# Mixer steps once per output block, with longer steps, a longer lead and one PSUM pool

## The chip, the cores and the metric

The kernel runs on one core of one Trainium2 chip. The metric is the device time of one execution in microseconds (us); lower is better. Times of the kernel before are the median of three runs.

The core's engines have short names here, as in the profile: PE is TensorE (its matmuls; PEld are its weight loads, which overlap matmuls), DVE is VectorE, ACT is ScalarE, POOL is GpSimd and SP is SyncE, which issues the DMAs. Each engine takes its instructions in a fixed order and waits at an instruction until its semaphores allow it.

## The reference

Two encoder layers over 272 rows (256 tokens and 16 learned meta tokens) of width 2048, in float32. Cut to what matters:

```python
def _layer(h, w_in, ...):
    proj = jnp.einsum('bld,dp->blp', h, w_in)
    gq, gk, gv, gr, glr, nq, nk, nv = jnp.split(proj, points, axis=-1)
    y_gla = _gla_mixer(gq, gk, gv, gr, glr, ...)      # 4 heads, both directions, gated linear attention
    y_na = _na_mixer(nq, nk, nv, na_rel_bias)         # 16 heads, windowed softmax attention
    mix = jnp.einsum('blm,md->bld', jnp.concatenate([y_gla, y_na], axis=-1), w_out)
    h = _layer_norm(DEEPNORM_ALPHA * h + mix, ln1_w, ln1_b)
    ff = jnp.einsum('blf,fd->bld', jnp.square(jax.nn.relu(jnp.einsum('bld,df->blf', h, w_ff1))), w_ff2)
    return _layer_norm(DEEPNORM_ALPHA * h + ff, ln2_w, ln2_b)
```

The meta rows are dropped from the output, so the second layer computes only 256 rows wherever it can.

## The kernel before, in words

**The large matmuls.** Nearly all the time goes to `x @ w` with weights streamed from HBM. Each product is made of three matmuls on rounded halves: high weight by high and low activation, and low weight by high activation (`three`, lines 169 to 180). A matmul has 128 output rows and 272 columns; with 256 columns, the first two are one matmul of 512. The streamed unit is a chunk of weights, 128 x 1024: DMA to `raw` (L164), ACT rounds it to `wh` (L165), DVE subtracts to get `wl` (L166). Three buffers of each rotate, and `weights` keeps one chunk ahead of the one in use. The chunk is eight k-blocks of one output block.

`by_m` (lines 208 to 223) makes one output block m after another in one PSUM bank from 16 k-blocks, which is two chunks: 48 matmuls of 272 columns. After each chunk and after the block's eviction it calls `pump`. `by_k` (lines 191 to 206) makes four blocks at once in four banks, two k-blocks for each chunk, and calls `before(k)` ahead of each chunk. The output projection starts with `by_k` over `self.y`, and there `before` is `mixed` (lines 310 to 316), which also calls `pump`.

**The mixers as generators.** Everything small is written as generators that run up to their next `yield` when `pump` steps them. `fg` holds the gates, the transposes of V, the silu of the GLA output gate, the neighbourhood attention pairs and the layer-norm sums; `bg` holds the GLA heads and the norm. `pump(fg, bg)` adds credits and does as many steps as there are whole credits. A step's instructions are traced under `issue_after(self.wl)`, which puts its DVE instructions behind the newest `wl`.

- `gla_head` (lines 467 to 573): nine levels of scores in the order 7, 0 to 6, 8. `operands(lv)` makes a level's decayed q and k on DVE (L491, L496) and ACT (L493, L495); the level's matmuls are L517 and L519, and DVE merges them into `A` under a mask (L524). The operands of a level are made one level ahead of its matmuls. Then come the meta keys (`across`, L532, L535), the outputs (L550 to L554), the mean of squares (`mean`, L788), the inverse root, the gate. It yields 16 times for a head, so about once for a level.
- `na_pair` (lines 599 to 674): two attention heads. Its parts are the scores (matmuls L610 and, in layer 0, L614) and their softmax (DVE adds L619, maximum L591, ACT exponentials L593, reciprocal L594, DVE products L597 that write `ns` and `npr`); in layer 0 the softmax of the meta queries (`nms`); the transposes of V (L631, L632); the transposes of the probabilities (L646, L647, L649) and their copies to SBUF; the output matmuls (L661, L666). There is a `yield` after each of the five.

In `layer` (lines 249 to 308) the four heads are queued in `bg` ahead of the two groups of the output gate (`ev_r`); then six groups of four blocks make the neighbourhood q, k and v (`ev_na`), a pair's three blocks one after another, and a pair is queued in `fg` when its v block is evicted. `bg` is emptied ahead of the sixth group. The last pair is queued by the last block, right ahead of the output projection's `by_k`.

**Layer norm sums.** In `tail` the output blocks are added into `acc` by `ln_part`. At block 3 it sums four blocks (L762, L763) and steps `ln_shift` once, which rounds the sum for a matmul with ones (`sp`: ACT L226, DVE L227); the next pump gives the matmul itself (`mean`, L788).

**PSUM.** Eight banks, in two pools of four: `pm` for the large products (tag `mm`) and `pb` for everything else (`bank`, tag `bg`). A pool hands out its banks in turn, in the order in which the program asks. The order of each engine's instructions is set by a list scheduler at build time, which may move an instruction past others when its own estimates say that it would wait.

Of the kernel before, what the change touches and what calls it, by code (L numbers as in the profile page):

```python
# [14 lines left out]
P = 128  # L15
# [3 lines left out]
NM = 16  # L19
# [12 lines left out]
EPS = 1e-5  # L32
TAU = 16.0
NEG = -1e30
GLA_R, GLA_NA, NORMS = 1.3, 1.1, (1.0, 0.6)
LEAD = 4
DIF = 1
HALVES = slice(0, T // 2), slice(T // 2, T)


# [13 lines left out]
class Trunk:  # L54
    def __init__(self, ctx, tc, ins, out):
        self.ctx, self.tc, self.nc = ctx, tc, tc.nc
        self.i, self.out = ins, out
        self.bg, self.fg, self.credit, self.fcredit = deque(), deque(), 0, 0
        self.x = [None] * DC
        self.stream, self.ready = self.order(), deque()  # L60
        pool = lambda name, **k: ctx.enter_context(tc.tile_pool(name=name, **k))
        self.cp = pool("const", bufs=1)
        self.xp = pool("xhl", bufs=1)
        self.yp = pool("yhl", bufs=1)
        self.wp = pool("wst", bufs=3)
        self.jp = pool("jn", bufs=1)
        self.pm = pool("pm", bufs=4, space=PSUM)
        self.pb = pool("pb", bufs=4, space=PSUM)

    def bank(self):  # L70
        return self.pb.tile([P, 512], F32, name="bg", tag="bg")

    def consts(self):
        nc, c = self.nc, self.cp
# [130 lines left out]
                                      start=j + p == 0, stop=j == nk - 1 and p == 2)  # L205
        return [p[:, :n] for p in ps]

    def by_m(self, acts, ns, evict, pump=(0, 0), apart=False, renew=False):

        nk = len(acts)  # L210
        for m, n in enumerate(ns):
            ps = self.pm.tile([P, 512], F32, name="mm", tag="mm")
            for k in range(nk):
                if k % 8 == 0:
                    wh, wl = self.weights()
                self.three(ps, wh, wl, (k % 8) * P, acts[k], n, k == 0, k == nk - 1)
                if k % 8 == 7 and k < nk - 1:
                    self.pump(*pump)
                if renew and m == len(ns) - 1 and k == 8:
                    self.renew(2)  # L220
            parts = [ps[:, :T], ps[:, T:]] if n == T else [ps[:, :n]]
            evict(m, parts if apart else self.whole(parts))
            self.pump(*pump)
# [25 lines left out]
    def layer(self, l):  # L249
        nc, tc = self.nc, self.tc  # L250
        self.l = l
        self.full = l + 1 < DEPTH
        self.n = n = L if self.full else T
        with ExitStack() as actx:
            pool = lambda name, side, ctx=actx, bufs=1: ctx.enter_context(
                tc.tile_pool(name=name, bufs=bufs, side=side, reuse_waits="tile"))
            a = pool("att", "left")
            t = lambda nm, s: a.tile(s, F32, name=nm, tag=nm)
            self.qk = [t(f"qk{h}", [P, 2, L]) for h in range(GH)]
            self.be = [t(f"be{h}", [P, 2, L + 1]) for h in range(GH)]  # L260
            self.nb = [t(f"nb{h}", [P, 4]) for h in range(GH)]
            self.V = [t(f"V{i}", [P, GH * GDV]) for i in range(2)]
            self.VS = a.tile([80, GH * GDV], F32R, name="VS", tag="VS")
            nc.gpsimd.memset(self.VS.bitcast(F32), 0.0)
            self.y, self.gate, self.done = [None] * DC, {}, set()
            if l:
                self.by_m(self.x, [L + 2] * 4, lambda m, ps: self.fixed(self.ev_k, m, ps), pump=(1, NORMS[0]),
                          renew=True)
                first = self.by_k(self.x, L, self.normed)
                self.drain()  # L270
                self.lctx.close()
            else:
                with ExitStack() as ectx:
                    self.xr = pool("xr", "right", ectx)
                    for m, ps in enumerate(self.by_k(self.x, L, self.load_x, fine=True)):
                        self.ev_k(m, ps)
            with ExitStack() as ectx:
                self.ep = pool("early", "right", ectx)
                self.fcredit = 0
                self.fg.append(self.gates())  # L280
                if l == 0:
                    self.by_m(self.x, [L] * 4, self.ev_v, pump=(1, 0))
                else:
                    for m, ps in enumerate(first):
                        self.ev_v(m, ps)
                self.by_m(self.x, [n] * 4, self.ev_q, pump=(1, 0))
                self.by_m(self.x, [L] * 4, lambda m, ps: self.ev_v(4 + m, ps), pump=(1, 0))
                self.drain()
            self.a2 = pool("na", "left", bufs=2)
            with ExitStack() as gctx:  # L290
                self.credit = 0
                self.g2 = pool("gla", "right", gctx, 2)
                for h in range(GH):
                    self.bg.append(self.gla_head(h))
                for g in range(2):
                    self.by_m(self.x, [n] * 4, lambda m, ps: self.ev_r(4 * g + m, ps), pump=(1, GLA_R))
                self.na_tiles()
                for g in range(6):
                    if g == 5:
                        while self.bg:  # L300
                            self.step(self.bg, 1)
                        gctx.close()
                        self.ln_open()
                    ns = [n if (4 * g + m) % 3 == 0 else L for m in range(4)]
                    self.by_m(self.x, ns, lambda m, ps: self.ev_na(4 * g + m, ps), pump=(1, GLA_NA))
            ps = self.by_k(self.y, n, self.mixed)
            self.drain()
        self.tail(ps)
# [157 lines left out]

    def gla_head(self, h):
        nc, n, full, g2 = self.nc, self.n, self.full, self.g2
        be, qk = self.be[h], self.qk[h]
        bf, eb = be[:, 0, 1:], be[:, 1, :]  # L470
        A = g2.tile([P, 6, P], F32, name="A", tag="A")
        Am = g2.tile([NM, L], F32, name="Am", tag="Am")
        level = lambda: g2.tile([P, 2, L], F32, name="lev", tag="lev", bufs=3)

        def flat(t):

# [30 lines left out]
            return t  # L507

        order = (7, 0, 1, 2, 3, 4, 5, 6, 8)
        ahead = operands(order[0])  # L510
        for at, lv in enumerate(order):
            q, k = ahead
            ahead = operands(order[at + 1]) if at + 1 < len(order) else across()
            ps = self.bank()
            for b in (slice(0, P), slice(P, T)):
                r = b if lv < 8 else slice(P - b.start, T - b.start)
                nc.tensor.matmul(ps[:, b], lhsT=k[:, b], rhs=q[:, r], start=True, stop=True)  # L517
            if full and lv <= 4:
                nc.tensor.matmul(ps[:, T:L], lhsT=k[:, T:T + P], rhs=q[:, T:L], start=True, stop=True)  # L519
            p2 = ps[:, :T].rearrange("p (s c) -> p s c", s=2)  # L520
            if lv >= 7:
                nc.scalar.copy(A[:, 0:5:4, :] if lv == 7 else A[:, 1:4:2, :], p2)
            else:
                nc.vector.copy_predicated(A[:, 0:5:4, :], self.mask[:, lv:lv + 1, :].to_broadcast([P, 2, P]), p2)  # L524
            if full and lv == 0:
                nc.vector.tensor_copy(Am[:, T:L], ps[:NM, T:L])
            elif full and lv <= 4:
                nc.vector.copy_predicated(Am[:, T:L], self.mask[:NM, lv, :NM], ps[:NM, T:L])
            yield
        t = ahead  # L530
        ps = self.bank()
        nc.tensor.matmul(ps[:, :T], lhsT=flat(t)[:, T:T + P], rhs=t[:, 1, :T], start=True, stop=True)  # L532
        if full:
# [2 lines left out]
                                 rhs=t[:, 1, T:L], start=True, stop=True)  # L536
            nc.vector.tensor_copy(A[:, 2:6:3, :NM], ps[:, T:T + 2 * NM].rearrange("p (s c) -> p s c", s=2))
        nc.scalar.copy(Am[:, :T], ps[:NM, :T])
        yield
        am = g2.tile([80, L], F32R, name="am", tag="am")[:, :n]  # L540
        nc.gpsimd.memset(am.bitcast(F32), 0.0)
        self.stack(Am[:, :n], am, NM, (0, 64), 32)
        yield
        af = A.rearrange("p s c -> p (s c)")
        os_ = []
# [19 lines left out]
        for e in range(2):  # L565
# [7 lines left out]
            yield  # L573

    def na_tiles(self):

# [22 lines left out]
    def na_pair(self, c, q, k, v):  # L599
# [24 lines left out]
        yield  # L624
# [15 lines left out]
        yield  # L640
# [509 lines left out]
```

## Time and profile before

| | |
|---|---|
| median of 3 runs | 2365.45 us (2365.10 to 2365.86) |
| the profiled execution | 2365.56 us |
| its span, first to last instruction | 2363.8 us |
| PE busy | 2339.4 us, 99% of the span, 17354 matmuls |
| PEld busy | 2228.2 us, 94% |
| DVE busy | 1570.9 us, 66% |
| ACT busy | 1239.3 us, 52% |
| granted TensorE clock, mean | 0.998 |

The times outside the span are 1.76 us. The profile's page gives busy shares for each engine and a chain of waits followed back from the end; the timeline gives each instruction's start, duration, engine, line, tiles and, in brackets, the idle time ahead of it with what ended it. Matmuls are pipelined, so the distance between two starts, not the duration, is what one costs. The two stages with the mixers' background steps lie at about 114 to 360 us (layer 0) and 1313 to 1553 us (layer 1).

### The profile page before, as it was taken

The page shows a single profiled execution, that of the slowest core. Times are in us where ns is not written, and L with a number is a line of the kernel's source. Part 1 is how long each engine was busy: PE and PEld are TensorE (multiplying, and loading weights), DVE is VectorE, ACT ScalarE, POOL GpSimd, SP SyncE. Part 2 cuts the span into 40 slices and gives each one's busy share as a digit, 9 for nine tenths or more (in the row PEclk, how much of TensorE's full clock was granted, in tenths as well). Part 3 has the DMA queues.
Part 4 walks back from the last instruction along what each step waited for, and adds up shares of the span by engine and source line. Part 5 has one row for each costly group of instructions (what it writes and reads, how often), then busy time and mean ns, then how long its engine had stood idle before and what let it go on. Part 6 is the DMA issues. An engine that isn't in the chain of part 4 may idle for free.

```text
span 2363.8 us, 43168 instructions
## 1 busy us (share of the span) xinstructions
PE 2339.4 (99%) x17354; PEld 2228.2 (94%) x17354; DVE 1570.9 (66%) x2474; ACT 1239.3 (52%) x2251; POOL 109.8 (5%) x181
## 2 busy tenths in 40 slices
PE   9999999999999999999999999999999999999997
PEld 8999999999999999999999899998988888888887
DVE  6697777785544455547577887768866555666656
ACT  6566665564433344444456677655654333444444
POOL 1100010020000000000021000000200000000001
PEclk9999999999999999999999999999999999999999
DMA  7544445555555555556556454456566666666664
GB/s 250 165 136 150 152 141 161 176 179 181 179 179 179 180 181 181 181 179 179 179 173 190 150 157 148 147 157 199 183 193 194 196 191 193 195 193 192 195 193 137
DMA packets 120425, 417.47 MB, mean 177 GB/s; under 512 B 13405, under 2 KB 18397, under 8 KB 120225
## 3 DMA queue, kind: packets, MB, share of 16 engines
q1 hardware_dynamic: 120224, 414.72, 56.5%
q8 instruction: 136, 2.23, 0.4%
q14 instruction: 65, 0.52, 0.1%
HBM read 412.57 MB, written 2.10 MB: 175 GB/s over the span
## 4 chain that ended last, share of the span: by engine, by line
PE 95%; DVE 3%; ACT 1%; issue 1%; DMA 0%; SPq 0%; ACTq 0%; DVEq 0%
PE mm L174 21%; PE mm L178 17%; PE mm L179 17%; PE mm L180 17%; PE mm L175 11%; PE mm L204 6%; PE bg L517 2%; PE bg L661 1%; DVE wl L166 1%; PE bg L610 0%; ACT wh L165 0%; PE bg L550 0%; PE bg L351 0%; PE mm L943 0%; PE mm L958 0%
## 5 line engine op out<-in xcount | busy, mean ns | idle before, releaser
L166 DVE TENSOR_TENSOR wl<-raw,wh 128x1024 fp32r<-128x1024 f32 (+1 forms) x764 | 931.2, 1219 | 638.0 <-ACT wh L165 625.8
L165 ACT CAST wh<-raw 128x1024 fp32r<-128x1024 f32 (+1 forms) x764 | 796.5, 1043 | 929.7 <-PE mm L179 378.3
L178 PE MATMUL mm<-x,wh 128*128 128x272 f32 (+2 forms) x2176 | 622.5, 286 | 0.0
L179 PE MATMUL mm<-x,wh 128*128 128x272 f32 (+2 forms) x2176 | 618.6, 284 | 0.0
L180 PE MATMUL mm<-x,wl 128*128 128x272 f32 (+2 forms) x2176 | 617.7, 284 | 0.1
L179 PEld LDWEIGHTS mm<-x,wh 128*128 128x128 f32 x2176 | 408.7, 188 | 0.1
L178 PEld LDWEIGHTS mm<-x,wh 128*128 128x128 f32 x2176 | 407.7, 187 | 1.1 <-issue 0.5
L180 PEld LDWEIGHTS mm<-x,wl 128*128 128x128 f32 x2176 | 407.7, 187 | 0.5 <-DVE wl L166 0.3
L174 PE MATMUL mm<-x,wh 128*128 128x512 f32 x1152 | 396.8, 390 | 0.0
L175 PE MATMUL mm<-x,wl 128*128 128x256 f32 x1152 | 318.6, 277 | 0.0
L174 PEld LDWEIGHTS mm<-x,wh 128*128 128x128 f32 x1152 | 216.3, 188 | 45.2 <-issue 0.6
L174 PE MATMUL mm<-y,wh 128*128 128x512 f32 x672 | 230.5, 388 | 0.7 <-ACT wh L165 0.7
L175 PEld LDWEIGHTS mm<-x,wl 128*128 128x128 f32 x1152 | 216.2, 188 | 0.0
L178 PE MATMUL mm<-y,wh 128*128 128x272 f32 x704 | 199.2, 283 | 0.0
L179 PE MATMUL mm<-y,wh 128*128 128x272 f32 x704 | 199.2, 283 | 0.0
L180 PE MATMUL mm<-y,wl 128*128 128x272 f32 x704 | 198.9, 283 | 0.0
L175 PE MATMUL mm<-y,wl 128*128 128x256 f32 x672 | 184.5, 275 | 0.7 <-DVE wl L166 0.7
L174 PE MATMUL mm<-u,wh 128*128 128x512 f32 x480 | 164.6, 388 | 0.0
L174 PEld LDWEIGHTS mm<-y,wh 128*128 128x128 f32 x672 | 126.1, 188 | 27.1 <-ACT wh L165 1.2
L178 PE MATMUL mm<-u,wh 128*128 128x272 f32 x512 | 144.9, 283 | 0.0
L179 PE MATMUL mm<-u,wh 128*128 128x272 f32 x512 | 144.9, 283 | 0.0
L180 PE MATMUL mm<-u,wl 128*128 128x272 f32 x512 | 144.7, 283 | 0.0
(262 smaller groups left out, 3272.1 us busy)
## 6 DMA issues: line engine op xcount, KB each, us to landing
raw<-in_wff SPq DMA_DIRECT2D x512, 512.0 KB, 3.6
raw<-in_win SPq DMA_DIRECT2D x190, 512.0 KB, 3.6
raw<-in_wout SPq DMA_DIRECT2D x64, 512.0 KB, 3.6
nb<-in_nab SPq DMA_DIRECT2D x16, 352.0 KB, 3.2
xraw<-in_xT SPq DMA_DIRECT2D x7, 272.0 KB, 5.0
out<-acc SPq DMA_DIRECT2D x7, 256.0 KB, 2.4
wraw<-in_wup SPq DMA_DIRECT2D x2, 392.0 KB
raw<-in_win SPq DMA_DIRECT2D x4, 128.0 KB, 2.8
```

Source lines behind the costliest of these rows:

```text
L165: nc.scalar.copy(wh[:, c], raw[:, c])
L166: self.wl = nc.vector.tensor_tensor(wl[:, c], raw[:, c], wh[:, c].bitcast(F32), ALU.subtract).ins
L174: mm(ps, lhsT=wh[:, c:c + P], rhs=x.joined, start=first, stop=False)
L175: mm(ps[:, T:], lhsT=wl[:, c:c + P], rhs=xh[:, :T], start=False, stop=last)
L178: mm(o, lhsT=wh[:, c:c + P], rhs=xh[:, :n], start=first, stop=False)
L179: mm(o, lhsT=wh[:, c:c + P], rhs=xl[:, :n], start=False, stop=False)
L180: mm(o, lhsT=wl[:, c:c + P], rhs=xh[:, :n], start=False, stop=last)
L204: self.nc.tensor.matmul(ps[m][:, :n], lhsT=parts[p][0][:, c:c + P], rhs=acts[j][parts[p][1]][:, :n], start=j + p == 0, stop=j == nk - 1 an ...
L517: nc.tensor.matmul(ps[:, b], lhsT=k[:, b], rhs=q[:, r], start=True, stop=True)
L661: nc.tensor.matmul(r[hs], lhsT=(v2 if rest else v1)[:, t, hs], rhs=p2[:, t, :] if rest else p1[:, 2 * t + hh, :], start=rest, stop=not rest)
```

## The change

- `by_m` gets `whole`: with it there is no pump after a block's first chunk, only the one after its eviction. The eight groups of the mixer stages use it, with `pump=(1, 1)`: one step of `fg` and one of `bg` for each block.
- Steps are longer. A GLA head yields 7 times instead of 16: four steps of two levels each, one with the last level, `across` and the meta scores, one with the outputs and the sums of squares, one with the mean, the root and both gated outputs. `na_pair` yields 3 times instead of 5: scores with all the softmax; transposes of V and of the probabilities; outputs.
- Operands are made for two levels at a time, at the end of the step ahead of the one that uses them; the first two of head 0 ahead of the first group, those of the next head within the fifth step of a head. One generator for the heads chains to the next (`yield from head`).
- `lev` gets 4 buffers and `dif` 2; `A`, `Am` and `am` get 1.
- The two PSUM pools become one pool of eight banks with one tag.

The diff, cut:

```diff
-GLA_R, GLA_NA, NORMS = 1.3, 1.1, (1.0, 0.6)
+NORMS = 1.0, 0.6
-DIF = 1
+DIF = 2
...
-        self.pm = pool("pm", bufs=4, space=PSUM)
-        self.pb = pool("pb", bufs=4, space=PSUM)
+        self.pm = pool("pm", bufs=8, space=PSUM)
 
     def bank(self):
-        return self.pb.tile([P, 512], F32, name="bg", tag="bg")
+        return self.pm.tile([P, 512], F32, name="bg", tag="mm")
...
-    def by_m(self, acts, ns, evict, pump=(0, 0), apart=False, renew=False):
+    def by_m(self, acts, ns, evict, pump=(0, 0), apart=False, renew=False, whole=False):
...
-                if k % 8 == 7 and k < nk - 1:
+                if k % 8 == 7 and k < nk - 1 and not whole:
                     self.pump(*pump)
...
-                for h in range(GH):
-                    self.bg.append(self.gla_head(h))
+                head = self.gla_head(0)
+                next(head)
+                self.bg.append(head)
                 for g in range(2):
-                    self.by_m(self.x, [n] * 4, lambda m, ps: self.ev_r(4 * g + m, ps), pump=(1, GLA_R))
+                    self.by_m(self.x, [n] * 4, lambda m, ps: self.ev_r(4 * g + m, ps), pump=(1, 1), whole=True)
...
-                    self.by_m(self.x, ns, lambda m, ps: self.ev_na(4 * g + m, ps), pump=(1, GLA_NA))
+                    self.by_m(self.x, ns, lambda m, ps: self.ev_na(4 * g + m, ps), pump=(1, 1), whole=True)
...
         order = (7, 0, 1, 2, 3, 4, 5, 6, 8)
-        ahead = operands(order[0])
+        ahead = [operands(lv) for lv in order[:2]]
+        yield
...
         for at, lv in enumerate(order):
-            q, k = ahead
-            ahead = operands(order[at + 1]) if at + 1 < len(order) else across()
+            q, k = ahead.pop(0)
             ps = self.bank()
...
-            yield
-        t = ahead
+            if not ahead and at < 8:
+                ahead = [operands(order[i]) if i < 9 else across() for i in (at + 1, at + 2)]
+                yield
+        t = ahead.pop()
...
         self.stack(Am[:, :n], am, NM, (0, 64), 32)
+        head = self.gla_head(h + 1)
+        next(head, None)
         yield
...
             self.done.add(c)
-            yield
+        yield
+        yield from head
...
         self.softmax(s, st, 4, ((s[:, :, :P], s[:, :, :P]), (pr[:, :, :NK2], s[:, :, P:])))
-        yield
         if self.full:
             mt = b.tile([NM, 6], F32, name="mst", tag="mst")
             self.softmax(sm, mt, 2, ((sm, sm),))
...
                 nc.scalar.copy(v2[hh * 64:hh * 64 + NK2, t, hs],
                                pv[t * 64:t * 64 + NK2, T + hh * NAD:T + hh * NAD + NAD])
-        yield
         p1 = b.tile([P, 4, P], F32, name="p1", tag="p1", bufs=1)
```

Where it moves instructions on PE. The first place is the end of layer 0's mixers: the last pair's scores and the start of the output projection (`mm<-y`, the number of y is a buffer's). Before, PE's order there, from the last matmul of the last v block on (line numbers of before):

```order
L180 MATMUL mm<-x_393,wl 128x272
L610 MATMUL bg<-nk,nq 128x176 x4
L614 MATMUL bg<-nk,nq 128x48 x2
L204 MATMUL mm<-y_1518,wh 128x272
L204 MATMUL mm<-y_1518,wl 128x272
L204 MATMUL mm<-y_1518,wh 128x272
L204 MATMUL mm<-y_1616,wh 128x272
```

The transposes of this pair stand further on: those of V after 24 matmuls of the projection, those of the probabilities (`ns`) after 51. With the change (its own line numbers: L614 and L618 are the scores, L634 and L635 the transposes of V, L648 to L651 those of the probabilities, L203 the projection):

```order
L614 MATMUL bg<-nk,nq 128x176 x4
L618 MATMUL bg<-nk,nq 128x48 x2
L634 MATMUL bg<-ident,nv_2209 128x128 x2
L635 MATMUL bg<-ident,nr_2210 128x128
L648 MATMUL bg<-ident,ns 128x128 x2
L649 MATMUL bg<-ident,npr_2214 128x128
L648 MATMUL bg<-ident,ns 128x128 x2
L649 MATMUL bg<-ident,npr_2214 128x128
L651 MATMUL bg<-ident,nms_2222 128x128
L203 MATMUL mm<-y_1509,wh 128x272
```

The pair's second step now stands directly behind its first, ahead of the projection: the first is pumped after the last block, the second by `mixed(0)`. The same stands at the end of layer 1's mixers.

The second place is the sums of the second layer norm, here in layer 1, where block 4's products with `y` and `u` follow block 3's. Before, the mean's matmul (`sp`, `onesr512`) on PE:

```order
L175 MATMUL mm_25296<-y10_23232,wl_25298 128x256
L174 MATMUL mm_25296<-y11_23233,wh_25299 128x512
L175 MATMUL mm_25296<-y11_23233,wl_25298 128x256
L788 MATMUL bg_25291<-sp0_25288,onesr512_487 128x256
L174 MATMUL mm_25296<-y12_23234,wh_25299 128x512
```

With the change:

```order
L174 MATMUL mm_25188<-u31_23250,wl_25234 128x256
L790 MATMUL bg_25288<-sp0_25285,onesr512_484 128x256
L173 MATMUL mm_25293<-y0_23219,wh_25257 128x512
L174 MATMUL mm_25293<-y0_23219,wl_25256 128x256
L790 MATMUL bg_25288<-sp0_25285,onesr512_484 128x256
```

It stood 24 matmuls into block 4 (behind y0 to y11); now it stands ahead of block 4's first matmul. Its bank (`bg_25288`) is asked for ahead of block 4's (`mm_25293`), which with one pool come from the same turn. Layer 0's second norm has the same: 25 matmuls into the block before, none now. The two first norms stand where they stood.

More of the change, by code (lines that the diff above doesn't have):

```diff
@@ L468, in gla_head @@
         nc, n, full, g2 = self.nc, self.n, self.full, self.g2
+        if h == GH:
+            return
         be, qk = self.be[h], self.qk[h]
         bf, eb = be[:, 0, 1:], be[:, 1, :]
-        A = g2.tile([P, 6, P], F32, name="A", tag="A")
-        Am = g2.tile([NM, L], F32, name="Am", tag="Am")
-        level = lambda: g2.tile([P, 2, L], F32, name="lev", tag="lev", bufs=3)
+        level = lambda: g2.tile([P, 2, L], F32, name="lev", tag="lev", bufs=4)
         def flat(t):
@@ L509, in gla_head @@
         order = (7, 0, 1, 2, 3, 4, 5, 6, 8)
-        ahead = operands(order[0])
+        ahead = [operands(lv) for lv in order[:2]]
+        yield
+        A = g2.tile([P, 6, P], F32, name="A", tag="A", bufs=1)
+        Am = g2.tile([NM, L], F32, name="Am", tag="Am", bufs=1)
         for at, lv in enumerate(order):
-            q, k = ahead
-            ahead = operands(order[at + 1]) if at + 1 < len(order) else across()
+            q, k = ahead.pop(0)
             ps = self.bank()
@@ L538, in gla_head @@
         nc.scalar.copy(Am[:, :T], ps[:NM, :T])
-        yield
-        am = g2.tile([80, L], F32R, name="am", tag="am")[:, :n]
+        am = g2.tile([80, L], F32R, name="am", tag="am", bufs=1)[:, :n]
         nc.gpsimd.memset(am.bitcast(F32), 0.0)
         self.stack(Am[:, :n], am, NM, (0, 64), 32)
+        head = self.gla_head(h + 1)
+        next(head, None)
         yield
@@ L572, in gla_head @@
             self.done.add(c)
-            yield
+        yield
+        yield from head
     def na_tiles(self):
@@ L623, in na_pair @@
         self.softmax(s, st, 4, ((s[:, :, :P], s[:, :, :P]), (pr[:, :, :NK2], s[:, :, P:])))
-        yield
         if self.full:
@@ L639, in na_pair @@
                                pv[t * 64:t * 64 + NK2, T + hh * NAD:T + hh * NAD + NAD])
-        yield
         p1 = b.tile([P, 4, P], F32, name="p1", tag="p1", bufs=1)
```

## Prediction

> **What bounds the kernel now.** I read the page first: the span, the busy shares, the chain.
>
> ```profile
> span 2363.8 us, 43168 instructions
> PE 2339.4 (99%) x17354; PEld 2228.2 (94%) x17354; DVE 1570.9 (66%) x2474; ACT 1239.3 (52%) x2251; POOL 109.8 (5%) x181
> PE 95%; DVE 3%; ACT 1%; issue 1%; DMA 0%; SPq 0%; ACTq 0%; DVEq 0%
> ```
>
> PE is the bound: busy 99% and 95% of the chain. The change does not alter PE's instructions, only their order. So time can come only from what PE waits, and from what switching between large products and steps may cost. Next I read the two mixer stages in the table of windows (length, then busy us of PE, PEld, DVE, ACT, POOL, then clock and DMA).
>
> ```profile
> 114.00:360.00 246.00, 245.17 (x2067) 239.60 (x2066) 195.56 (x403) 163.99 (x445) 18.07 (x35) 1.00 0.46 143
> 1313.00:1553.00 240.00, 239.13 (x1743) 219.13 (x1742) 194.99 (x359) 167.03 (x445) 13.87 (x35) 1.00 0.49 150
> ```
>
> PE is idle for 246.00 - 245.17 = 0.83 and 240.00 - 239.13 = 0.87 us there, 1.7 us together, because a waiting matmul still overlaps the drain of the one before. The weight loads show more of the waits. In layer 0 PEld is idle 6.4 us. In layer 1 it is idle 20.9 us, but there the matmuls of 512 columns are longer than their loads, so that figure is no wait. The view of waits names the producers (us in total, times, longest):
>
> ```profile
> PEld bg L517 <- DVE lev L496: 1.6, 4, 0.7
> PEld bg L788 <- ACT sp L226: 1.1, 4, 0.3
> PEld bg L788 <- ACT p L651: 0.9, 2, 0.5
> PEld bg L646 <- DVE gtn L463: 0.5, 2, 0.3
> ```
>
> These sum to 4.1 us. Nothing larger is there to win.
>
> **Fewer interruptions.** Counted in PE's order, the background matmuls break the large products 171 times before and 113 times after. The price of one break is read from a timeline in layer 0's mixers: starts, durations, and seven transposes between two products.
>
> ```profile
> 251.60 0.29 PE L180 MATMUL mm<-x,wl 128*128 128x272 f32 x1
> 251.72 0.38 PE L646 MATMUL bg<-ident,ns 128*128 128x128 f32 x2
> 252.38 0.27 PE L649 MATMUL bg<-ident,nms 128*128 128x128 f32 x1
> 252.40 0.37 PE L178 MATMUL mm<-x,wh 128*128 128x272 f32 x1
> 252.61 0.29 PE L179 MATMUL mm<-x,wh 128*128 128x272 f32 x1
> ```
>
> From 251.60 to 252.61 is 1.01 us. It holds two large matmuls at 0.12 us from start to start (251.60 to 251.72) and seven transposes at (252.38 - 251.72) / 6 = 0.11. That is 0.24 + 0.77 = 1.01, so a break itself costs nothing, and 58 fewer save about 0 (at most the last digit, 0.01 us each, 0.6 us).
>
> **The waits in the stages.** A level's operands now have a whole block (48 products at 0.12 us, about 5.9 us) instead of a chunk, but two levels are made in it. I take the four rows above as won: -4 us; bounds -1.7 (PE's idle time) and -7 (layer 0's 6.4 us and the last digits).
>
> **The last pair, layer 0.** After the change nothing stands between the last pair's scores and its transposes but three transposes of V (the order above). PE must sit out the softmax, which 51 products of the output projection cover now:
>
> ```profile
> 358.93 0.87 PE L610 MATMUL bg<-nk,nq 64*128 64x176 f32 x8
> 359.88 0.39 PE L204 MATMUL mm<-y,wh 128*128 128x272 f32 x1
> 360.34 1.15 POOL L431 COPY nr<-nv 128x32 f32<-128x32 f32 x2 [6.08 <-ACT nv L427]
> 362.37 0.88 DVE L591 TENSOR_REDUCE nst<-ns 128x4 f32<-128x704 f32 x1
> 363.21 1.05 ACT L165 CAST wh<-raw 128x1024 fp32r<-128x1024 f32 x1 [2.84 <-issue]
> 364.16 0.44 ACT L593 ACTIVATE ns<-ns,nst 128x176 f32<-128x176 f32 x1
> 366.22 0.69 DVE L597 TENSOR_TENSOR ns<-ns,nst 128x512 f32<-128x512 f32 x1
> 367.06 0.52 PE L646 MATMUL bg<-ident,ns 128*128 128x128 f32 x3 [0.25 <-DVE ns L597]
> ```
>
> The scores end where the first `y` product starts, 359.88. Three transposes (0.33) would bring PE to 360.21 (the third also waits for POOL's copies, which end at 361.49; that lies inside the longer wait). `ns` is ready at 366.22 + 0.69 = 366.91. In that chain the exponentials begin at 364.16, behind a cast of weights whose buffer the projection's own matmuls set free. With PE waiting that cast comes later, so the exponentials can begin when the maximum is there, 362.37 + 0.88 = 363.25, 0.91 us earlier: `ns` at 366.0. The wait is 366.0 - 360.2 = 5.8, plus some 0.2 for `npr` and `nms`, which come last, less the 0.25 that PE waits now: **+5.7 us**. Bounds: 4.5 (if the weights' subtraction ahead of the scores' add on DVE moves away too) and 6.5.
>
> **The last pair, layer 1.** The same without meta queries:
>
> ```profile
> 1551.74 0.87 PE L610 MATMUL bg<-nk,nq 64*128 64x176 f32 x8
> 1552.54 0.39 PE L204 MATMUL mm<-y,wh 128*128 128x256 f32 x1
> 1554.75 0.88 DVE L591 TENSOR_REDUCE nst<-ns 128x4 f32<-128x704 f32 x1
> 1556.62 0.44 ACT L593 ACTIVATE ns<-ns,nst 128x176 f32<-128x176 f32 x1
> 1558.68 0.69 DVE L597 TENSOR_TENSOR ns<-ns,nst 128x512 f32<-128x512 f32 x1
> ```
>
> PE would be free at 1552.54 + 0.33 = 1552.87. `ns` comes at 1558.68 + 0.69 = 1559.37, less 1556.62 - (1554.75 + 0.88) = 0.99 for the exponentials' earlier start: 1558.4. **+5.5 us**, bounds 4.4 and 6.3.
>
> **The second norms.** The mean's matmul is now ahead of block 4's first product (the order above; the shared pool hands block 4's bank out behind the mean's). PE waits for the sum of block 3 and its rounding. Layer 0, then layer 1:
>
> ```profile
> 1069.55 0.28 PE L178 MATMUL mm<-y,wh 128*128 128x272 f32 x1
> 1072.79 0.39 PE L788 MATMUL bg<-sp,onesr 128*128 128x272 f32 x1
> ```
>
> ```profile
> 2214.89 0.39 PE L174 MATMUL mm<-y,wh 128*128 128x512 f32 x1
> 2217.66 0.42 DVE L763 TENSOR_TENSOR s<-s,s 128x256 f32<-128x256 f32 x1
> 2218.65 0.40 ACT L226 CAST sp<-s 128x256 fp32r<-128x256 f32 x1
> ```
>
> Layer 0: the rounded sum lets the matmul go at 1072.79; block 4's first product, which it now precedes, went at 1069.55. That is 3.24 less one product's 0.12, and less 0.2 that PE loses there now: **+2.9**. Layer 1: the sum is there at 2217.66 + 0.42 = 2218.08. The cast runs at 2218.65 now, behind a weights' cast that PE's later matmuls release, so it can start at 2218.1 and end at 2218.5: 2218.5 - 2214.9 - 0.1 = **+3.5**. Bounds for each: 2.0 (no subtraction of weights, 1.2 us, inside the sum) and 3.7. The second half of the rounding follows two or three products later and costs nothing more.
>
> **The other seven pairs of a layer.** Scores and probabilities stand a block apart now; before it was 1.5 blocks. By the rows above the chain from the scores' start to `ns` is 366.0 - 358.93 = 7.1 us in layer 0; PE has 0.95 for the scores, 5.9 for the block and 0.33 for V, 7.2 us, and 0.4 to 0.7 more where levels stand there too. That is just enough on an undisturbed DVE, and DVE is busy 195.56 of 246 us. I take 0.15 us for each of 14 pairs, **+2**; bounds 0 and 10 (0.7 each, one subtraction of half a chunk's length).
>
> **The sum**, against the profiled execution's 2365.56: 5.7 + 5.5 + 2.9 + 3.5 - 4 + 2 = +15.6, 2381.2. That execution is 0.11 us above the median of 2365.45, so the forecast is 2381. The ends: all lower bounds give 4.5 + 4.4 + 2 + 2 - 7 + 0 = +5.9; all upper ones 6.5 + 6.3 + 3.7 + 3.7 - 1.7 + 10 = +28.5. Both extremes at once are unlikely; the likeliest case's own range is 2374 to 2388.
>
> **Rivals.**
>
> *PE cools in the waits (slower, 2385).* The window rows after the last matmul (2350.1) show the granted clock as the third number from the end:
>
> ```profile
> 2350.50:2352.80 2.30, 0.00 (x0) 0.00 (x0) 1.45 (x4) 1.80 (x8) 2.30 (x4) 1.00 0.43 124
> 2352.80:2355.00 2.20, 0.00 (x0) 0.00 (x0) 2.10 (x5) 0.84 (x3) 1.48 (x3) 0.50 0.56 164
> ```
>
> and at the start four products take 0.91 us, and later four take 0.50:
>
> ```profile
> 6.02 1.11 PE L204 MATMUL mm<-x,wl 128*128 128x272 f32 x4
> 6.93 1.57 PE L204 MATMUL mm<-x,wh 128*128 128x272 f32 x8
> 8.34 0.66 PE L204 MATMUL mm<-x,wl 128*128 128x272 f32 x4
> 8.84 0.41 PE L204 MATMUL mm<-x,wh 128*128 128x272 f32 x2
> ```
>
> So the clock halved 2.7 us after the last matmul, and at the start PE ran at about half speed until somewhere between 6.93 and 8.34. A wait of about 5 us can do the same; then some 3 to 4 us run at half speed, 1.7 us lost each time. In the two long waits that is +3.4. Against it: PE takes the transposes of V in between. [...]
>
> *The softmax is late for every pair (slower, 2391).* If DVE's extra work ahead of each softmax takes 0.7 us more than the cover, 14 x 0.7 = 10 us come on top instead of 2. For it: 7.1 against 7.2 us. Against it: PE's idle time in the stages is only 1.7 us now with DVE as busy.
>
> *The stages gain more than the new waits cost (faster, 2359).* Longer lead and eight banks could end all waits of the stages, -7 us. The point that decides: the four new waits would have to cost less than that together, which means that the last pair's softmax and the norms' sums are done when PE arrives. Rows for that are missing: the softmax's own instructions from maximum to `ns` take 366.0 - 362.4 = 3.6 us. [...]
>
> *The new waits are covered or offset (no change, 2366).* The lead gives -7 and the four waits stay under 7 us. It shares the last rival's objection.
>
> **How the numbers follow.** Chances: the forecast 0.68 (2381), cooling 0.14 (2385), late softmax 0.10 (2391), no change 0.05 (2366), faster 0.03 (2359). A change of 0.2%, 4.7 us, is about what a measurement of this kernel can tell from none. Slower by more: 0.68 + 0.14 + 0.10 = 0.92; within 0.05; faster 0.03. The range 2374 to 2389 holds the first two cases up to the unlikely ends and a part of the third.
>
> **What would show it.** Right: in the new trace PE waits 5 to 6 us ahead of L648 at the start of each output projection, and 2.5 to 3.7 us ahead of L790 at the start of block 4 in both second norms; the sum of the other waits in the stages is no more than now. Wrong: products between scores and transposes there, a softmax done within 3 us, or waits for `wl` or `lev` of more than 5 us in the stages.

## The result, and the profile after

The changed kernel takes 2389.0 us (median of 4 runs, 2388.32 to 2391.3) against 2365.27 us for the kernel before (4 runs, 2364.45 to 2365.86). The ratio is 1.0102 (95% interval 1.009 to 1.0114): slower by 23.7 us, where the forecast had 15.6 us and a range up to 2389 us. The profiled execution of the changed kernel is the longest of its four, 2391.3 us; against before's 2365.56 it lost 25.7 us. The profile is read against that figure.

The page of the changed kernel has the same number of matmuls, and DVE and ACT are as busy as before. PE is busy 8 us longer, and the chain of waits has moved from PE to DVE and ACT:

```profile
span 2389.5 us, 43164 instructions
PE 2347.1 (98%) x17354; PEld 2236.2 (94%) x17354; DVE 1571.0 (66%) x2474; ACT 1237.5 (52%) x2251; POOL 104.6 (4%) x181
PE 93%; DVE 4%; ACT 2%; issue 1%; DMA 1%; SPq 0%; ACTq 0%; DVEq 0%
```

PE does the same work in 2347.1 instead of 2339.4 us: some of it ran slower. The rest is waiting. The view of PE's waits names it; these are its largest rows for the transposes of `ns` and the norms' mean (us in total, times, longest):

```profile
PE bg L648 <- DVE ns L601: 9.7, 3, 4.7
PE bg L790 <- ACT sp L225: 6.6, 2, 3.5
PE bg L648 <- ACT jn L186: 1.0, 1, 1.0
```

The first two rows hold the two long waits (and a third of 0.7 us) and the two norm waits of the forecast. Here is the first of them in the timeline, layer 0's last pair (start, duration, engine, line, in brackets the idle time before and who ended it):

```profile
361.07 0.44 PE L634 MATMUL bg<-ident,nv 128*128 128x128 f32 x2 [0.38 <-ACT nv L427]
362.27 0.33 PE L635 MATMUL bg<-ident,nr 128*128 128x128 f32 x1 [0.77 <-POOL nr L431]
363.11 0.88 DVE L595 TENSOR_REDUCE nst<-ns 128x4 f32<-128x704 f32 x1
364.02 0.44 ACT L597 ACTIVATE ns<-ns,nst 128x176 f32<-128x176 f32 x1 [0.25 <-DVE nst L595]
366.08 0.69 DVE L601 TENSOR_TENSOR ns<-ns,nst 128x512 f32<-128x512 f32 x1
366.92 0.66 PE L648 MATMUL bg<-ident,ns 128*128 128x128 f32 x2 [4.31 <-DVE ns L601]
368.29 0.57 PE L203 MATMUL mm<-y,wh 128*128 128x272 f32 x1
...
1572.95 0.66 PE L648 MATMUL bg<-ident,ns 128*128 128x128 f32 x2 [4.71 <-DVE ns L601]
```

(The last row is the same place in layer 1.) The exponentials start right behind the maximum, as the forecast had it, and PE waits for the softmax with nothing to do. But the durations behind the wait are new. Two transposes took 0.38 us before; they take 0.66. The first `y` product takes 0.57 instead of 0.39. The table of windows shows why. Its stretches are cut where the clock record changes, and 3.41 us from there (length, then busy us of PE, PEld, DVE, ACT, POOL, then the granted clock, DMA share and GB/s):

```profile
362.03:365.45 3.42, 0.33 (x1) 0.14 (x1) 2.10 (x7) 2.52 (x12) 0.19 (x2) 1.00 0.53 155
365.45:368.86 3.41, 1.95 (x9) 1.98 (x10) 1.45 (x5) 1.74 (x9) 0.00 (x0) 0.50 0.00 0
368.86:372.27 3.41, 3.41 (x17) 3.41 (x16) 0.17 (x1) 0.36 (x2) 0.00 (x0) 0.50 0.00 0
1078.83:1082.24 3.41, 0.87 (x7) 0.87 (x8) 2.51 (x5) 0.84 (x2) 0.00 (x0) 1.00 0.58 159
1082.24:1085.66 3.42, 3.42 (x18) 3.42 (x17) 2.94 (x6) 1.65 (x5) 0.00 (x0) 0.50 0.36 140
1085.66:1089.07 3.41, 3.41 (x30) 3.41 (x29) 3.31 (x9) 2.52 (x5) 0.00 (x0) 1.00 0.00 0
1566.94:1570.35 3.41, 0.82 (x5) 0.34 (x3) 2.99 (x5) 1.98 (x9) 0.36 (x2) 1.00 0.38 143
1570.35:1573.77 3.42, 0.82 (x4) 0.85 (x5) 1.14 (x3) 1.52 (x8) 0.00 (x0) 0.50 0.45 145
1573.77:1577.18 3.41, 3.41 (x18) 3.41 (x17) 0.00 (x0) 1.08 (x4) 0.00 (x0) 0.50 0.00 0
2235.95:2239.36 3.41, 0.14 (x1) 0.14 (x2) 2.78 (x6) 1.13 (x2) 0.00 (x0) 1.00 0.68 173
2239.36:2242.78 3.42, 3.42 (x12) 2.94 (x13) 2.05 (x4) 0.51 (x2) 0.00 (x0) 0.50 0.33 134
```

Behind all four waits the granted clock is 0.50, behind the two norms' as well: in 1082.24 to 1085.66 PE is busy without a break over 18 matmuls, 0.23 us from start to start, in the next stretch, at full clock, over 30, 0.12 us from start to start. Behind the long waits the record stays at half for two stretches; in the first of the two PE is busy for 1.95 and 0.82 us only. At half clock PE worked 372.27 - 366.92 = 5.35, 3.41, 1577.18 - 1572.95 = 4.23 and 3.42 us. By the record's 0.50, half of these 16.4 us, 8.2, would be lost, as an estimate.

The mixer stages themselves gained nothing (before: 245.17 and 239.13 us busy; layer 1's window is shifted by 14 us, as it starts about 13 us later):

```profile
114.00:360.00 246.00, 245.10 (x2070) 240.11 (x2070) 195.69 (x403) 162.20 (x445) 16.34 (x36) 1.00 0.46 144
1327.00:1567.00 240.00, 237.73 (x1732) 217.97 (x1730) 193.00 (x358) 165.00 (x443) 12.35 (x36) 1.00 0.49 150
```

Both traces hold the same products of the projections, apart from a few places in the same order. The start of one product in both therefore shows what was lost up to it. For example, layer 0's first `y` product went at 359.88 and goes at 368.29. Taken so at the borders of the stages, where no step's matmuls are outstanding, the 25.8 us divide as follows (with the column of the experiment `e4_warm`, below, where PE is kept busy in the four waits):

| place | lost | forecast | lost with PE kept busy |
|---|---|---|---|
| ahead of layer 0's mixers | 0.5 | 0 | 0.3 |
| layer 0's mixers | 0.3 | mixers together -2 | 0.3 |
| last pair, layer 0 | 7.9 | 5.7 | 5.5 |
| second norm, layer 0 | 4.5 | 2.9 | 2.8 |
| layer 1's mixers | 1.3 | | 2.2 |
| last pair, layer 1 | 7.1 | 5.5 | 5.2 |
| output projection, layer 1 | -0.9 | 0 | -0.9 |
| second norm, layer 1 | 5.1 | 3.5 | 3.0 |

### The profile page after: what moved, and what is told of

Same layout as the page of the kernel before. It is cut to its first block, busy times and chain, and to the rows that moved or that the text cites. A ratio compares the mean times of both kernels' runs of the same rounds, so it can differ in the third digit from the quotient of the medians.

```text
span 2389.5 us, 43164 instructions
## 1 busy us (share of the span) xinstructions
PE 2347.1 (98%) x17354; PEld 2236.2 (94%) x17354; DVE 1571.0 (66%) x2474; ACT 1237.5 (52%) x2251; POOL 104.6 (4%) x181
## 4 chain that ended last, share of the span: by engine, by line
PE 93%; DVE 4%; ACT 2%; issue 1%; DMA 1%; SPq 0%; ACTq 0%; DVEq 0%
PE mm L173 21%; PE mm L177 17%; PE mm L178 17%; PE mm L179 17%; PE mm L174 10%; PE mm L203 6%; DVE wl L165 1%; PE bg L519 1%; DMA raw<-in_win 1%; PE bg L663 1%; ACT wh L164 1%; PE bg L614 0%; PE bg L648 0%; PE bg L555 0%; PE mm L945 0%
```

## The experiments

Each is compared with the kernel before on the same chip (medians there 2365.68, 2365.04 and 2364.91 us for the three groups of runs). "+n" is the difference to that. The change itself is +23.7.

**Two theories of the cause.** Theory B is the prediction's: the last pair waits because its second step is longer and is pumped right behind its first, whatever the pools; only the norms are the pool's doing. Theory A: the one pool makes all four waits. With two pools the scheduler is free to put a step's matmuls among later products on PE, and with one PE's order follows the order in which banks are asked for.

**The pools alone undone** (`e1_two_pools`):

```diff
-        self.pm = pool("pm", bufs=8, space=PSUM)
+        self.pm = pool("pm", bufs=4, space=PSUM)
+        self.pb = pool("pb", bufs=4, space=PSUM)
...
-        return self.pm.tile([P, 512], F32, name="bg", tag="mm")
+        return self.pb.tile([P, 512], F32, name="bg", tag="bg")
```

> The changed kernel with its PSUM banks in two pools of four again; steps, operands and pumps stay as changed. Theory A (the one pool is what holds PE at all four places: with its own pool a step's matmuls may stand among later products, and PE's order now has the last pair's probability transposes 44 and 45 products into the output projections, and the mean's 25 and 24 products into block 4): all four waits and the half-speed stretches behind them go, 7.9 + 4.5 + 7.1 + 5.1 = 24.6 us of the two profiles' 25.7, so 2364 to 2367, and no record of half speed before the last matmul. Theory B (the prediction's: the last pair waits because its second step is pumped right behind its first, whatever the pools): only the norms' 4.5 + 5.1 = 9.6 us go, 2379, and two half-speed records stay.

Measured: 2369.78 us, +4.1 (ratio 1.0017, 1.0008 to 1.0026). All four waits are gone although the steps are as changed; the clock record shows no half speed before the last matmul. Theory B falls: without the one pool the merged steps make no wait. The timeline of the same place shows the reason: 44 products of the projection (L204) stand between the scores and the transposes of the probabilities (L649), and PE doesn't wait for the softmax.

```profile
361.08 0.44 PE L635 MATMUL bg<-ident,nv 128*128 128x128 f32 x2 [0.38 <-ACT nv L428]
361.27 0.37 PE L204 MATMUL mm<-y,wh 128*128 128x272 f32 x1
...
362.29 0.33 PE L636 MATMUL bg<-ident,nr 128*128 128x128 f32 x1
...
366.55 0.66 PE L204 MATMUL mm<-y,wl 128*128 128x272 f32 x4
367.05 0.38 PE L649 MATMUL bg<-ident,ns 128*128 128x128 f32 x2
```

The remaining +4.1 was not expected. Most of it lies in layer 1's mixers (+3.4 in the trace, +1.2 in layer 0's). PE's view, here over both layers, names ACT's copies of a pair's V (L642) ahead of matmuls that don't read them, so these are most likely waits for a bank:

```profile
PE bg L537 <- ACT nv L642: 0.9, 2, 0.4
PE bg L649 <- ACT nv L642: 0.7, 2, 0.3
PE bg L520 <- ACT nv L642: 0.7, 2, 0.4
```

**The pool alone done** (`e5_before_one_pool`): the kernel before with the opposite edit.

> The kernel before with one pool of eight banks and nothing else changed. Theory A: the two norms' waits come with their half-speed stretches, 4.5 + 5.1 = 9.6 us, so 2375; the last pairs keep 24 and 51 products between their steps, which are pumped apart, and gain no wait. A rival (eight banks give the stages more room, as the prediction's faster rival had it): the stages gain up to 4 us against that, 2371.

Measured: 2392.41 us, +26.7 (1.0113, 1.0099 to 1.0127). Both theories missed: 17 us more than the norms. The pool alone costs more than the whole change. The norms wait as foreseen. The last pairs don't wait (0.0 us in the trace at both places): their steps are pumped apart here, and in layer 0 24 products of the projection stand ahead of V's transposes and 27 more ahead of those of the probabilities. So the last pairs' waits need both halves of the change, the one pool and the merged steps, and theory A holds as it stands for the norms alone. The levels wait too, and behind one of these waits, 3.36 us that end at 1380.87, the granted clock is 0.50 from 1382.35 (rows in the last section); over the whole span it is 0.995, in the kernel before 0.998. The likely reason, which no run tests by itself, is that before's steps make a level's operands only one step ahead, and PE's order no longer lets the level's matmuls drift behind later products:

```profile
PE bg L516 <- DVE lev L495: 13.9, 10, 3.4
PE bg L787 <- ACT sp L225: 6.6, 2, 3.5
```

So what the new steps are worth depends on the pools. With one pool they save some 3 us (26.7 to 23.7): in the traces the mixers lose 1.6 instead of some 19 us, and the last pairs 15.0 instead of nothing. With two pools they cost 4.1.

**The last pair's second step later** (`e2_later`), one pool kept:

```diff
     def mixed(self, k):
-        self.pump(1, 0)
+        if k > 2:
+            self.pump(1, 0)
```

> The changed kernel, one pool, but the output projection pumps from its third pair of chunks on, so that the last pair's second step stands 48 products behind its first. Theories A and B alike: both long waits and their half-speed stretches go, 7.9 + 7.1 = 15.0 us, so 2374; the norms' two waits stay, with two half-speed records of 3.4 us. A rival (the softmax of a last pair is late anyway, as DVE and ACT are full at the start of the projection): 2 to 3 us of each wait stay, 2379.

Measured: 2375.39 us, +9.7 (1.0041, 1.0025 to 1.0056). The long waits and their half-speed stretches are gone; the trace's loss to before is 0.0 us at both places, and 4.5 and 5.2 us remain at the norms. The rival (a softmax late anyway) falls.

**The banks asked for in another order** (`e7_one_pool_later`): the same, and the second norms' mean asks one step later.

```diff
         self.split(src, *parts)
         yield
+        if late:
+            yield
         p = self.bank()[:, :src.shape[-1]]
...
-        p = yield from self.mean(self.s2, 4 * P)
+        p = yield from self.mean(self.s2, 4 * P, late=which == 1)
```

> The changed kernel with its one pool, but its banks asked for in another order: the output projection pumps from its third pair of chunks on, as in the run before, and the second norms' mean asks for its bank one step later, so that its matmul stands 24 to 25 products into block 4 again. Theory A (the one pool costs only where a step asks for its bank ahead of products that could cover its wait): the 9.6 us of the norms go on top of the 13.6 that the later second step brought, 2375.4 - 9.6 = 2365.8, 2364 to 2368, and no half-speed record before the end. A rival (sharing eight banks costs by itself, by evictions that products wait for): 3 us or more stay above that.

Measured: 2365.66 us, +0.6 (1.0002, 0.9993 to 1.0011), not to be told from before. So sharing eight banks costs nothing by itself; where the two steps stand costs it all. That it is the order of asking for banks that binds PE is argued, not shown. Both edits move a step's matmuls in the program together with its requests, and at the last pairs `by_k` asks for the projection's four banks (L193 of the kernel before) ahead of `mixed(0)`, so there the step's matmuls come first in the program, but not its requests. Of the waits that are left, PE's view has these for transposes:

```profile
PE bg L649 <- DVE ns L602: 1.1, 3, 0.7
PE bg L405 <- ACT ft L396: 1.0, 1, 1.0
PE bg L649 <- ACT jn L186: 1.0, 1, 1.0
```

**PE kept busy in the waits** (`e4_warm`): products of zeros on top of the change, into the bank that the step takes anyway.

```diff
+    def idle(self, ps, n):
+        for _ in range(n):
+            self.nc.tensor.matmul(ps[:, :T], lhsT=self.ones_r[D], rhs=self.VS0, start=True, stop=True)
...
             pt = self.bank()
+            if c == 7 and not t:
+                self.idle(pt, 36)
...
         p = self.bank()[:, :src.shape[-1]]
+        if warm:
+            self.idle(p, 24)
```

> The changed kernel with 36 products of zeros on PE in each of the two long waits (about 4.4 us at 0.121 us) and 24 in each of the two norm waits (2.9 us); their results are overwritten and change no output. If PE's halved clock behind the waits is a cost of its own: the waits stay, the half-speed records go, and of (5.35 + 3.41 + 4.23 + 3.41) / 2 = 8.2 us most comes back, 2381 to 2382. If the slow products behind the waits have another cause (late weights, transfers): 2389, or more by what the products of zeros exceed the waits.

Measured: 2383.67 us, +18.0 (1.0075, 1.0061 to 1.0089): 120 products more, and 5.3 us less than the changed kernel in the medians (some 2 us above what was expected), 7.5 between the two profiled executions (2391.3 and 2383.83). Of that difference 24.7 - 16.5 = 8.2 us come from the four places (the table's last column); 0.9 are lost again in layer 1's mixers, where PE waits 1.1 us for a `wl` as it doesn't in the changed kernel. The stretch behind the first long wait now has the full clock:

```profile
364.94:368.36 3.42, 2.57 (x23) 2.40 (x22) 1.45 (x5) 2.31 (x12) 0.00 (x0) 1.00 0.01 4
368.36:371.77 3.41, 3.41 (x41) 3.24 (x39) 0.17 (x1) 1.04 (x2) 0.00 (x0) 1.00 0.02 5
```

No half speed is on record before the last matmul. At the two last pairs PE still waits for `ns` behind the zeros (0.85 and 0.61 us), so the zeros don't lengthen these waits, and what comes back there, some 2.4 and 1.9 us, is the clock's. At the two norms the test is less clean: the 24 products take some 2.9 us (at 0.12 us each), block 4's first products go right behind them, ahead of the mean's, and PE doesn't wait for `sp` at all. So 2.8 and 3.0 us there are the length of the zeros. What the clock costs at a norm is read better from `e5_before_one_pool` (last section): the same wait of 3.51 us costs 3.5 us at full clock and 5.1 with the half-speed stretch behind it.

The halved clock is a cost of its own, about a third of what each of the four places lost.

**The steps divided**, on two pools: only the three-step pairs (`e8_before_pairs`: before, without the two `yield`s, `pump=(0.5, GLA_NA)`), and only the levels (`e9_levels`: the two pools of the first experiment, the two `yield`s back, `pump=(1.67, 1)` in the six later groups).

> The kernel before, two pools, with only the three-step attention pairs (half a step for each half block, so one for each block as changed); levels and operands as before. It divides the 4.1 us that the changed steps cost with two pools. If the pairs make them (a pair's V copies and softmax in fewer, longer steps on ACT, for which PE waited in that run): 2369 to 2370. If the levels make them (two levels' operands at once on DVE and ACT, for which the weights' subtraction comes late): 2365 to 2366.

> The changed kernel with two pools and five-step pairs as before (1.67 steps for each block, so a pair still takes three blocks); levels and operands as changed. The other half of the division: if the pairs make the 4.1 us, 2365 to 2366; if the levels do, 2369 to 2370; if each gives a part, this and the run with the pairs alone share them, about 2367 to 2368 each.

Measured: 2369.95 us, +4.9 (1.0022, 1.0014 to 1.0031), and 2369.86 us, +4.8 (1.0019, 1.001 to 1.0027). In the medians the costs don't add: each part alone costs as much as both. Neither theory holds. The waits differ: for the levels' operands in the first (2.5 us in six waits), for ACT's copies of the probabilities in the second. Behind the longest of these, 2.2 us, the granted clock is 0.50:

```profile
PE bg L666 <- ACT p L656: 3.9, 6, 2.2
254.98:258.40 3.42, 1.24 (x17) 0.99 (x17) 1.46 (x3) 2.31 (x6) 1.01 (x2) 1.00 0.53 207
258.40:261.81 3.41, 3.41 (x23) 3.19 (x19) 0.42 (x1) 0.83 (x3) 0.00 (x0) 0.50 0.57 154
```

A stretch of 3.41 us at 0.50 costs some 1.7 us, as an estimate. This trace is the longest of its 11 executions, 2372.24 us; the five shortest take 2367.4 to 2368.3. Over the 11 the mean granted clock lies between 0.996 and 0.998. So part of the levels' +4.8 is the clock's, and differs from one execution to the next. The 4 us belong to no single part; what the steps' rhythm has to do with two pools of four is not shown.

**A dose of banks** (`e12_six_banks`): the kernel of `e7_one_pool_later` with `bufs=6`.

> The kernel with one pool and its banks asked for later, with six banks instead of eight: a dose of the resource by itself. If eight banks are worth something in the mixer stages (the two pools of four with the changed steps took 4.1 us more, and PE waited there for copies by ACT that free banks): 3 us or more slower, 2369 or above. If banks were never short: the same, 2365.7.

Measured: 2373.38 us, +8.5 (1.0035, 1.0022 to 1.0049), 7.9 more than the +0.6 of the same kernel with eight. PE now waits for copies that free banks, ahead of large products too:

```profile
PE bg L793 <- ACT nv L642: 2.6, 2, 1.4
PE mm L177 <- ACT nv L642: 1.2, 3, 0.5
```

Eight banks are not too many here. Sharing them in one pool is another matter: that cost 26.7 us with the steps of before, and nothing with the new steps and two of them later.

**Towards a better version.** In `e7_one_pool_later` waits of about 1 us remain. On top of it `e10_adds` holds back the residual's sums on DVE; `e11_adds_swap` also puts the second V group ahead of the q group; `e13_before_adds` is the first edit on the kernel before.

```diff
-            self.nc.vector.tensor_tensor(self.acc[:, c, :self.n], h, lo, ALU.add)
+            with self.tc.issue_after(self.wl):
+                self.nc.vector.tensor_tensor(self.acc[:, c, :self.n], h, lo, ALU.add)
```

> The kernel with one pool and its banks asked for later, and besides the 16 sums of x's halves for the residual (acc<-x on DVE) of each layer issued no earlier than the weights' subtraction of their place. In that kernel six or more of these sums lie on DVE between the scores and ns of the pair before the last, and PE waits 0.86 us (344.23) and 1.16 us (1537.80) for that pair's ns. If the sums make these waits: 1.5 to 2 us less, 2364. If the subtractions of weights and ACT make them: no difference, 2365.7; if the later sums hold up the output's add instead: 2366 to 2367.

> The same, with the second group of V products ahead of the q products, so that the last transposes of V rows stand behind q blocks, whose copies are long done, instead of right behind their own block. With one pool PE waits 1.17 us there in layer 0 (109.10). Expected: 1.2 us less than the run with the sums alone, 2362.8, and 2 us or so under the kernel before; a rival (the levels' first operands, which need q, come as much later as q does): no gain.

> The kernel before with the sums of x's halves held back in the same way and nothing else changed. It shows whether what the run with one pool gains from that edit belongs to the changed steps or was to be had before. The kernel before waits 0.4 us for ns there (once): 2365 or up to 0.5 us less.

Measured: 2365.14 us (+0.2; 1.0, 0.9992 to 1.0009), 2364.48 us (-0.4; 0.9998, 0.9989 to 1.0007) and 2365.06 us (+0.2; 1.0001, 0.9992 to 1.0009). The sums were not what the pair before the last waited for: of the 2.1 us for `ns` and `jn` 1.7 stay, in the view of waits, with the sums held back. The swap removes the wait for `ft`, but its forecast of 2362.8 is missed by 1.7 us: as its rival had it, PE waits longer for the levels' operands (1.2 us instead of 0.6). No version beats the kernel before by more than its measurement can tell; the best is 0.4 us under it.

## Why the prediction was wrong in size

- **What bounds the kernel, and "fewer interruptions cost and save nothing"**: held as far as the runs go. The matmuls are the same, and nothing in the result needs a price for a break.
- **The last pairs, +5.7 and +5.5**: right as waits. With PE kept busy the two places lose 5.5 and 5.2 us. The softmax chain was read correctly from the rows of before, with the exponentials' earlier start: `ns` was forecast for 366.0 in before's time, and less the delay of 0.7 us that the trace has by then it comes at 366.08 + 0.69 - 0.7 = 366.1.
- **The second norms, +2.9 and +3.5**: right as waits. The 4.5 and 5.1 us lost there, less 1.7 for one half-speed stretch each, are 2.8 and 3.4.
- **The step that failed: the sum left the clock out.** It stood as a rival with a chance of 0.14 and a price of 3.4 us, in the two long waits only. The clock was at 0.50 behind all four waits, for 8.2 us in this execution, 4.8 of them behind the two long waits and 3.4 behind the norms'. The rival's 1.7 us for each wait was half of some 3 to 4 us at half speed; in before's trace PE works from 4.50 us on and at full speed from somewhere between 6.93 and 8.34, which is 2.4 to 3.8, and the record here has 3.41 us behind a norm and 6.83 behind a long wait. The argument against it was that PE takes V's transposes in between; in layer 0 these filled 0.33 of the 3.42 us of the stretch ahead of the half-speed one. The norms' waits, forecast as 3.2 and 3.6 us, had no such price at all; in layer 0 PE was still busy for 0.87 of the 3.41 us there, and the clock fell all the same. The row at the end of before's trace has half clock 2.7 us after the last matmul began, 2.4 after its end. All four waits were longer, and the sum had reason to take the clock as a term of its own.
- **The other term that failed: the stages, -4 and +2.** Measured +0.3 and +1.3, and 0.9 back behind layer 1's. The +2 came, but in two places and not in fourteen (0.87 and 1.16 us between two starts beyond a transpose's 0.11). The -4 did not. It was read from idle weight loads; PE's own view of before has 1.2 us of waits in the two stages (0.7 for `lev`, 0.5 for `p`), so most of it was hardly there to win. The longer lead didn't win it on two pools either (+1.2 and +3.4 us in the mixers of `e1_two_pools`). With one pool the lead has another worth: without it the pool alone waits 13.9 us for the levels' operands.
- **What was right in number and half right in cause**: the last pairs' waits were put down to the merged steps and the pump of `mixed(0)`. The order shown ahead of the prediction was right, but it takes the pool as well: with two pools the same steps and the same pump give no wait, and with one pool and the steps of before there is none either.
- **The sum**: 16.5 (four waits, forecast 17.6) + 8.2 (clock, forecast 0) + 1.1 (the rest, forecast -2) = 25.8 in the profiled execution; 23.7 in the medians. That the clock costs less in the other executions would explain the 2 us; this is not shown: the mean granted clock reads 0.994 in all four, and one in its last digit is 2.4 us.

What stays open: which part of the 4 us that the new steps cost on two pools is shortage of banks. The waits name it and the dose of six banks agrees, but no run isolates it. And by which rule the scheduler keeps a step's matmuls in place when there is one pool: the runs show that it does, not why.

## What to carry over

PE's four waits of 3.07 to 4.71 us cost about half as much again here (8.2 us on 16.5), by the clock of 0.50 behind them. In other runs the clock was at 0.50 behind waits of 2.2 and 3.36 us too, and behind one of 3.51 us it stayed at 1.00. So a sum of PE's waits in this kernel needs that term, as a range, for every wait of such a length. Where a scheduler is free to reorder, a shared pool can be not only a resource but an order: before merging two pools, look at which small product then stands ahead of the large ones that covered its wait. Here moving two steps gave back all 23 us, with the pool and the steps as changed.

## What the runs showed of the hardware

In the changed kernel's trace every change of the clock record falls on one grid of 3.41 us, whatever the place of the wait: 365.45 and 372.27 are two steps apart, 1082.24 and 1085.66 one, and 365.45 and 1082.24 are 210. PE was not idle throughout in the stretch ahead of a half-speed one: it was busy there for 0.33, 0.87, 0.82 and 0.14 us at the four waits. In the kernel before with one pool, on the grid of its own record, a stretch with 1.48 of 3.41 us busy was followed by one at 0.50, and stretches with 1.49, 1.57 and 1.74 us by ones at 1.00:

```profile
1378.94:1382.35 3.41, 1.48 (x11) 1.47 (x12) 3.41 (x7) 2.66 (x7) 0.00 (x0) 1.00 0.69 223
1382.35:1385.77 3.42, 3.42 (x12) 2.85 (x12) 2.79 (x7) 1.23 (x5) 0.00 (x0) 0.50 0.56 153
160.38:163.79 3.41, 1.49 (x13) 1.28 (x11) 3.41 (x5) 1.82 (x5) 0.00 (x0) 1.00 0.34 98
163.79:167.21 3.42, 3.04 (x25) 3.07 (x26) 3.42 (x7) 2.26 (x7) 0.00 (x0) 1.00 0.83 234
2235.69:2239.10 3.41, 1.57 (x10) 1.14 (x8) 2.76 (x4) 1.04 (x1) 0.00 (x0) 1.00 0.67 217
2239.10:2242.51 3.41, 1.74 (x11) 1.57 (x12) 2.02 (x6) 0.78 (x2) 0.00 (x0) 1.00 0.61 221
2242.51:2245.93 3.42, 3.42 (x23) 3.03 (x22) 3.42 (x8) 2.21 (x5) 0.00 (x0) 1.00 0.02 5
```

The last three rows are layer 1's second norm again, with the same wait for `sp` as in the changed kernel (3.51 us in both traces). It lies across the border of two stretches there, the clock stayed at 1.00, and the wait cost 3.5 us instead of 5.1. So one length of wait had two prices. PE's busy time here is partly modelled, and no one value of it parts the stretches of all traces: at the end of `e8_before_pairs` 1.61 us busy were followed by half speed.

```profile
2352.69:2356.10 3.41, 1.61 (x11) 1.08 (x9) 2.93 (x7) 2.96 (x10) 2.29 (x4) 1.00 0.50 144
2356.10:2359.51 3.41, 0.00 (x0) 0.00 (x0) 2.50 (x6) 1.87 (x5) 2.69 (x5) 0.50 0.38 111
```
